# RWKV output normalisation as its own chain in a hand-ordered weave, with attention, gate and output work taken off the raised priority

## The chip, the cores and the metric

One core of one Trainium2 chip runs the whole program. The metric is device time in microseconds (us) per execution, the median of three runs. Before the change it is 2834.69 us (2834.21 to 2839.68).

## What is computed

Two layers of a Conformer-style block on 512 tokens of width 1024, all in float32: a SwiGLU feed-forward, a mixing sub-layer, and a second feed-forward. The mixing sub-layer adds three gated branches: RWKV-7 (8 heads of 64), gated linear attention, and 4-head attention to a fixed memory. The part that matters here is the RWKV head recurrence and its output:

```
def step(state, inp):
    r_t, w_t, k_t, v_t, kk_t, a_t = inp
    sa = einsum('bhvk,bhk->bhv', state, -kk_t)
    state = state * w_t + sa * (kk_t * a_t) + v_t * k_t
    return state, einsum('bhvk,bhk->bhv', state, r_t)
mean = y.mean(-1); var = mean((y - mean) ** 2)
yn = (y - mean) * rsqrt(var + RWKV_LN_EPS) * ln_w + ln_b
out = (yn + sum(r * k * r_k, -1) * v) * g
...
merged = einsum('bsjc,jcd,bsjd->bsd', branches, w_branch, sigmoid(u_gate))
x = x + merged @ w_out
```

## The kernel before

Activations lie with channels on the 128 partitions and 512 tokens along the free axis. Every large weight tile is loaded as float32 (`wraw`), split by ScalarE into a high part `whi` (L180) and by VectorE into a low part `wlo` (L181), and each product is three 128x128 by 128x512 matmuls (high-high, high-low, low-high). In the mixing sub-layer these stand on L295 (`pieces`).

The RWKV core is chunked: 64 tokens a chunk, four chunks a **half**, two halves for each of four **head pairs**, so eight halves (numbered 0 to 7 below) in each of two layers. A half passes through four stages:

- *gates* (`rwkv_gates`): for the first half of a pair a norm over the keys (`ksq`, L379 on TensorE, square root L387, reciprocals L397), then two small products (L382), tanh (L384, L385) and the factors `kk`, `a`, `G` (L388 to L399).
- *first* (`rwkv_first`): the factors `AR`, `KB` (L426 to L432), score products (L444), masks (L449), start of a triangular inverse.
- *inverse* (`rwkv_inverse`): rounds of VectorE transpose `X` (L521), product (L528), mask `W` (L531), product (L536), sum into `Z` (L537).
- *second* (`rwkv_second`): the state recurrence over the four chunks. Each chunk goes through three products with a hand-over after each: L580 then `qs` (L581, VectorE); L586 then `VU` (L587/L588, ScalarE); L592 then the state `S` (L598, VectorE, two halves of 64 rows). After four chunks the outputs are formed (L608) and added into `y` (L613, twice).

Then comes the output part, which is the same generator's tail: sum and mean of `y` (L616, L617), subtraction (L618), square on ScalarE (L620), sum (L622), an inverse square root by three Newton steps in 14 small GpSimd instructions (L624 to L631), multiplication into `y` (L632). After a pause in the order, TensorE transposes `y` (L638) and forms the output gate (L639), and ScalarE and VectorE finish (L641 to L649).

`weave` writes TensorE's order by hand. It keeps a running clock `now` in ns; each generator yields the TensorE time of what it just issued and a latency, and is not asked again until `now` has passed that latency plus a slack of 400. In between, `stream` supplies the large matmuls of the other two branches and of the projections, one at a time at 227 ns. Generators are asked in a fixed order: second, inverse, first, gates, attention heads. TensorE executes exactly this order. The other engines' orders come from a scheduler that sorts what is ready by priority; all the chains are issued under `high_priority(offset=100000)`, the large stream is not. Each engine then runs its list strictly in order, so an instruction that waits holds everything behind it.

The pause after the normalisation is `yield 5 * 218, 7500` (L634). Because the tail belongs to `rwkv_second`, the next half's recurrence begins only after this half's transposes.

Of the kernel before, what the change touches and what calls it, by code (L numbers as in the profile page):

```python
# [19 lines left out]
P = 128  # L20
# [59 lines left out]
class Net:  # L80
# [322 lines left out]
    def rwkv_first(self, hp, hf, r, k, v, kk, kh, a, G):  # L403
        nc, rw, t1 = self.nc, self.rw, self.t256
        N = 256
# [60 lines left out]
            nc.scalar.activation(by(AB[rows, :, rows]), ab, AF.Copy)  # L466
            nc.scalar.activation(by(AU[rows, :, rows.start // 2:rows.start // 2 + 32]), ab[:, :, :, 32:64], AF.Copy)
        nc.vector.tensor_tensor(Z, A4, self.c("eye").unsqueeze(1).to_broadcast([P, 4, 64]), ALU.add)
        rk = t1("t1", 2)
        nc.vector.scalar_tensor_tensor(rk, r, self.pcol("r_k", hp), kh, ALU.mult, ALU.mult)  # L470
        self.freed = 2 * hp + hf + 1
        yield 8 * 218, 3600
# [37 lines left out]
        bv = t1("bv", 2)  # L510
# [51 lines left out]
    def rwkv_second(self, hp, hf, E, AR, VU, u0, GR, Z, KBT, bv):  # L562
        nc, rw, t1 = self.nc, self.rw, self.t256
        N = 256
        cs = slice(hf * N, (hf + 1) * N)
        hc = slice(hp * P, (hp + 1) * P)
        y = t1("y")
        for c in range(4):
            g = hf * 4 + c
            p, par = c // 2, c % 2  # L570
# [39 lines left out]
        for par in range(2):  # L610
            rows = slice(par * 64, par * 64 + 64)
            yv = y[rows].rearrange("p (h t) -> p h t", h=4)
            nc.vector.tensor_tensor(yv, psy[rows].rearrange("p (h e t) -> p h e t", h=4, e=2)[:, :, par, :], yv, ALU.add)  # L613
        y4 = y.rearrange("p (h t) -> p h t", h=4)
        st = rw.tile([P, 4], F32, name="st", tag="st", bufs=2)
        nc.vector.reduce_sum(st, y4, AX.X)  # L616
# [13 lines left out]
            nc.gpsimd.tensor_scalar(tt, tt, -0.5, 1.5, ALU.mult, ALU.add)  # L630
            nc.gpsimd.tensor_tensor(rt, rt, tt, ALU.mult)  # L631
        nc.vector.tensor_tensor(y4, y4, rt.unsqueeze(2).to_broadcast([P, 4, 64]), ALU.mult)  # L632
        self.seconds = 2 * hp + hf + 1
        yield 5 * 218, 7500  # L634

        ps = self.small("f")
        for q in range(2):
# [2 lines left out]
        y = t1("t2", 2)  # L640
# [12 lines left out]
    def weave(self, rkv0, gl, restore, xa):  # L653


        now, slack = 0, 400
        ready, rkv, gated, query = {0: 3500}, {0: rkv0}, {}, {}
        self.inv, self.sec, inverted = {}, {}, 0
        self.freed = self.seconds = self.tails = 0

        def first_gates():
            for n in range(8):
                while n // 2 not in rkv or ready[n // 2] > now or self.freed < n:
                    yield None
                gated[n] = yield from self.rwkv_gates(n // 2, n % 2, *rkv[n // 2])

        def first():
            for n in range(8):
                while n not in gated or self.seconds < n - 1:
                    yield None  # L670
                yield from self.rwkv_first(n // 2, n % 2, *gated.pop(n))

        def inverse():
            nonlocal inverted
            for n in range(8):
                while n not in self.inv:
                    yield None
                yield from self.rwkv_inverse(*self.inv.pop(n))
                inverted = n + 1

        def second():
            for n in range(8):
                while n not in self.sec or inverted <= n:
                    yield None
                yield from self.rwkv_second(n // 2, n % 2, *self.sec.pop(n))
                self.tails = n + 1

        def heads():
            for j in range(2, 4):
                while j not in query:  # L690
                    yield None
                yield from self.xa_head(xa[0], j, query[j], *xa[1:])
                ready[-j] = 0

        def rest():
            part = self.branch_g(1, *gl, True, range(KD))
            query[2] = yield from self.xa_query(xa[0], 2)
            yield None
            for cost in part:
                yield cost  # L700
                if cost is None and 3 not in query and -2 in ready:
                    query[3] = yield from self.xa_query(xa[0], 3)
                    yield None
            yield from self.branch_g(2, *restore(), False, range(KD))
            early = [self.keep.tile([P, 4 * NMEM], F32, name="early", tag=n) for n in ("kT", "vm")]
            for m in range(4):
                gates.append((yield from self.gate_g(0, m, early[m // 2][:, (m % 2) * T:(m % 2 + 1) * T])))
                yield None

        def stream():  # L710
            fill = rest()
            for hp in range(1, 4):
                while self.freed < 2 * hp:
                    cost = next(fill)
                    while cost is not None:
                        yield cost
                        cost = next(fill)
                rkv[hp] = yield from self.rwkv_rkv(hp)
                ready[hp] = now + 3500
            for cost in fill:  # L720
                if cost is not None:
                    yield cost

        gates = []
        parts = [[g, 0] for g in (second(), inverse(), first(), first_gates(), heads())]
        big = stream()
        ends = 0
        while parts or big is not None:
            for part in parts:
                if part[1] > now:  # L730
                    continue
                try:
                    with self.tc.high_priority(offset=100000):
                        step = next(part[0])
                except StopIteration:
                    parts.remove(part)
                    break
                if step is not None:
                    now += step[0]
                    part[1] = now + step[1] + slack  # L740
                    break
            else:
                if big is None:
                    now = min(part[1] for part in parts) if parts else now
                    ends += 1
                    assert ends < 100
                    continue
                try:
                    now += next(big)
                except StopIteration:  # L750
                    big = None
        return gates
# [382 lines left out]
```

## Time and profile before

| | us |
|---|---|
| median of the runs | 2834.69 |
| the profiled execution's own time | 2841.49 |
| its span, first to last instruction | 2839.6 |
| around the span (2841.49 - 2839.6) | 1.9 |
| weave of layer 1 of 2, from the key norm to the last transpose | 588 to 960 |
| weave of layer 2 of 2, same | 1998 to 2364 |

The profile's sections give each engine's busy time, the chain that ended last, and groups of instructions by source line; PE is TensorE, DVE is VectorE, ACT is ScalarE and POOL is GpSimd. In the views of waits, a row reads "who <- for whom: us in total, times, longest". In the views by stretch, each row has the length, the busy time of each engine with its instruction count, and the granted share of the TensorE clock. A small float32 matmul in the program appears as two records in the trace, because it is run in two passes.

### The profile page before, as it was taken

To read this page: it belongs to the slowest core of one execution; us is meant where nothing else is said; L and a number is where in the kernel's file an instruction comes from. 1 tells how busy PE (TensorE), PEld (TensorE's weight loads), DVE (VectorE), ACT (ScalarE), POOL (GpSimd) and SP (SyncE) were. 2 spreads that over 40 slices of the span, in tenths; PEclk is the share of its full clock that TensorE was granted. 3 is DMA by queue.
4 is the path that set the end of the run, shared out by engine and by line. 5 is a ranking of instruction groups with operands and counts; after the bars stand their busy time and mean duration, and the time that the engine had idled before them with its cause. 6 is when DMAs were issued, how large, how long until landed. Compare 5 with 4: busy or idle time off the path is not lost.

```text
span 2839.6 us, 35473 instructions
## 1 busy us (share of the span) xinstructions
PE 2737.2 (96%) x13280; PEld 2247.1 (79%) x13280; DVE 1617.8 (57%) x2993; ACT 1152.3 (41%) x2079; POOL 72.6 (3%) x342
## 2 busy tenths in 40 slices
PE   8999999998989999999999999999999899999998
PEld 6888887777777788888888888877777688888886
DVE  6434446777677654444454344567777775544444
ACT  5323345554343443323343233465544334432332
POOL 0000000001010000000000000000010110000000
PEclk9999999999899999999999999999999999999999
DMA  5232332211111232232332323312111113322222
GB/s 184 93 99 97 106 133 79 93 54 60 53 53 51 98 123 96 89 104 97 97 111 87 106 97 111 127 67 90 66 54 58 60 54 101 118 97 92 102 92 87
DMA packets 91723, 258.04 MB, mean 91 GB/s; under 512 B 10464, under 2 KB 24832, under 8 KB 91552
## 3 DMA queue, kind: packets, MB, share of 16 engines
q1 hardware_dynamic: 91552, 255.79, 26.8%
q8 instruction: 104, 1.70, 0.2%
q14 instruction: 67, 0.55, 0.1%
HBM read 243.69 MB, written 12.06 MB: 90 GB/s over the span
## 4 chain that ended last, share of the span: by engine, by line
PE 88%; DVE 6%; ACT 2%; POOL 2%; issue 2%; DMA 0%; SPq 0%; DVEq 0%; POOLq 0%; ACTq 0%
PE ps_b L295 21%; PE ps_b L196 19%; PE ps_b L198 19%; PE ps_b L197 18%; PE ps_c L528 2%; PE ps_c L536 1%; DVE wlo L181 1%; PE ps_i L444 1%; PE ps_f L794 1%; PE ps_f L586 1%; PE ps_f L816 1%; DVE knrm L397 0%; POOL tt L628 0%; ACT whi L180 0%; PE ps_y L932 0%
## 5 line engine op out<-in xcount | busy, mean ns | idle before, releaser
L180 ACT ACTIVATE whi<-wraw 128x512 fp32r<-128x512 f32 (+1 forms) x874 | 544.0, 623 | 1165.2 <-PE ps_b L197 901.6
L181 DVE TENSOR_TENSOR wlo<-wraw,whi 128x512 fp32r<-128x512 f32 (+1 forms) x874 | 589.9, 676 | 483.7 <-ACT whi L180 475.6
L196 PE MATMUL ps_b<-xhi,whi 128*128 128x512 f32 x1424 | 556.2, 391 | 9.9 <-ACT xhi L206 7.7
L198 PE MATMUL ps_b<-xhi,wlo 128*128 128x512 f32 x1424 | 555.8, 390 | 0.1
L197 PE MATMUL ps_b<-xlo,whi 128*128 128x512 f32 x1424 | 555.8, 390 | 0.0
L295 PE MATMUL ps_b<-xhi,wlo 128*128 128x512 f32 x864 | 353.6, 409 | 12.9 <-DVE wlo L181 12.9
L295 PE MATMUL ps_b<-xlo,whi 128*128 128x512 f32 x864 | 355.7, 412 | 0.0
L295 PE MATMUL ps_b<-xhi,whi 128*128 128x512 f32 x864 | 351.1, 406 | 1.8 <-DVE gc L945 1.2
L196 PEld LDWEIGHTS ps_b<-xhi,whi 128*128 128x128 f32 x1424 | 266.5, 187 | 67.0 <-ACT xhi L206 7.7
L198 PEld LDWEIGHTS ps_b<-xhi,wlo 128*128 128x128 f32 x1424 | 266.5, 187 | 57.9 <-DVE wlo L181 0.8
L197 PEld LDWEIGHTS ps_b<-xlo,whi 128*128 128x128 f32 x1424 | 266.6, 187 | 57.5 <-DVE xlo L207 0.5
L196 PE MATMUL ps_b<-mhi,whi 128*128 128x512 f32 x704 | 277.5, 394 | 0.0
L198 PE MATMUL ps_b<-mhi,wlo 128*128 128x512 f32 x704 | 276.0, 392 | 0.0
L197 PE MATMUL ps_b<-mlo,whi 128*128 128x512 f32 x704 | 273.3, 388 | 0.0
L295 PEld LDWEIGHTS ps_b<-xhi,wlo 128*128 128x128 f32 x864 | 165.7, 192 | 48.0 <-DVE wlo L181 15.9
L295 PEld LDWEIGHTS ps_b<-xhi,whi 128*128 128x128 f32 x864 | 165.6, 192 | 40.1 <-issue 5.6
L295 PEld LDWEIGHTS ps_b<-xlo,whi 128*128 128x128 f32 x864 | 165.8, 192 | 31.6 <-issue 1.8
L198 PEld LDWEIGHTS ps_b<-mhi,wlo 128*128 128x128 f32 x704 | 132.1, 188 | 30.9
L197 PEld LDWEIGHTS ps_b<-mlo,whi 128*128 128x128 f32 x704 | 132.2, 188 | 29.5
L196 PEld LDWEIGHTS ps_b<-mhi,whi 128*128 128x128 f32 x704 | 132.3, 188 | 26.3
L271 DVE TENSOR_TENSOR fm<-ps_b,ft 128x512 f32<-128x512 f32 x88 | 60.9, 692 | 126.9 <-PE ps_b L198 126.9
L267 DVE TENSOR_TENSOR ft<-ps_b,rs 128x512 f32<-128x512 f32 x88 | 60.9, 692 | 126.0 <-PE ps_b L198 125.8
(299 smaller groups left out, 3334.2 us busy)
## 6 DMA issues: line engine op xcount, KB each, us to landing
wraw<-in_ffn_in_dram SPq DMA_DIRECT2D x176, 512.0 KB, 3.4
wraw<-in_w_main_dram SPq DMA_DIRECT2D x108, 512.0 KB, 3.5
wraw<-in_ffn_out_dram SPq DMA_DIRECT2D x64, 512.0 KB, 3.5
wraw<-in_ffn_out_dram SPq DMA_DIRECT2D x64, 192.0 KB, 2.3
wraw<-in_w_branch_dram SPq DMA_DIRECT2D x48, 256.0 KB, 2.5
wraw<-in_w_out_dram SPq DMA_DIRECT2D x16, 512.0 KB, 3.4
xd<-x SPq DMA_DIRECT2D x16, 256.0 KB, 2.2
wraw<-in_w_k_dram SPq DMA_DIRECT2D x8, 512.0 KB, 3.6
```

Source lines behind the costliest of these rows:

```text
L180: nc.scalar.activation(hi, r, AF.Copy)
L181: nc.vector.tensor_tensor(lo, r, hi.bitcast(F32), ALU.subtract)
L196: nc.tensor.matmul(ps, a[0], b[0], start=start, stop=False)
L197: nc.tensor.matmul(ps, a[0], b[1], start=False, stop=False)
L198: nc.tensor.matmul(ps, a[1], b[0], start=False, stop=stop)
L267: nc.vector.tensor_tensor(t, pp[0], rs, ALU.mult)
L271: nc.vector.tensor_tensor(m, pp[1], t, ALU.mult)
L295: self.nc.tensor.matmul(ps, w[k][a], xs[k][b], start=k + i == 0, stop=k == n - 1 and i == 2)
L444: nc.tensor.matmul(pss[j][:, c * P:(c + 1) * P], KBc[js, c, :], AR[js, c, :], start=True, stop=True)
L528: nc.tensor.matmul(ps[:, u, :], AB[:, u, :], X[:, u, :], start=True, stop=True)
L536: nc.tensor.matmul(ps[:, u, :], W[:, u, :], Z[:, u, :], start=True, stop=True)
L586: nc.tensor.matmul(psu[:, :P], Z[:, 2 * p:2 * p + 2, :].rearrange("p j t -> p (j t)"), qs, start=True, stop=True)
```

## The change

The tail of `rwkv_second` from the first sum onward becomes a generator `rwkv_out`, and a new loop `outputs()` in the weave drives it. The pause before the transposes becomes `yield 0, 12000`. Second of the next half no longer waits for this half's transposes; it waits for those of the half before (`self.tails < n - 1`), and `y` gets two buffers. The loops carry a priority offset each: second, inverse and first keep 100000, gates, attention heads and outputs get 0, which is issue order. The very first gates become due 6000 instead of 3500 after the start. The tile `t1` goes from two buffers to one. No instruction is added or removed. Line numbers after the change: the lines of `rwkv_second` up to L613 become one lower, the tail's L616 to L632 become L624 to L640, L638/L639 become L645/L646, and attention's L794 becomes L809.

```
-        rk = t1("t1", 2)
+        rk = t1("t1")
...
-        y = t1("y")
+        y = t1("y", 2)
...
+        self.out[2 * hp + hf] = y, bv
+        yield 5 * 218, 0
+
+    def rwkv_out(self, hp, hf, y, bv):
...
-        self.seconds = 2 * hp + hf + 1
-        yield 5 * 218, 7500
+        yield 0, 12000
...
-        ready, rkv, gated, query = {0: 3500}, {0: rkv0}, {}, {}
+        ready, rkv, gated, query = {0: 6000}, {0: rkv0}, {}, {}
...
-                while n not in self.sec or inverted <= n:
+                while n not in self.sec or inverted <= n or self.tails < n - 1:
                     yield None
                 yield from self.rwkv_second(n // 2, n % 2, *self.sec.pop(n))
+                self.seconds = n + 1
+
+        def outputs():
+            for n in range(8):
+                while n not in self.out:
+                    yield None
+                yield from self.rwkv_out(n // 2, n % 2, *self.out.pop(n))
                 self.tails = n + 1
...
-        parts = [[g, 0] for g in (second(), inverse(), first(), first_gates(), heads())]
+        parts = [[g, 0, p] for g, p in ((second(), 100000), (inverse(), 100000), (first(), 100000), (first_gates(), 0),
+                                        (heads(), 0), (outputs(), 0))]
...
-                    with self.tc.high_priority(offset=100000):
+                    with self.tc.high_priority(offset=part[2]):
```

Three places show what the edit does to the engines' lists, all in the first layer.

TensorE around the transposes of half 0, before. Here `ksq` and `wlal` are the gates of half 2, and L295 the large stream:

```order
L295 MATMUL ps_b<-yh,whi 128x512
L295 MATMUL ps_b<-yl,whi 128x512
L379 MATMUL ps_i<-ksq,cst 128x512
L382 MATMUL ps_i<-wlal,wz 128x256 x2
L638 MATMUL ps_f<-cst,y 128x128 x2
L639 MATMUL ps_f<-sgl,g_1111 128x256
L295 MATMUL ps_b<-yh,wlo 128x512
L295 MATMUL ps_b<-yh,whi 128x512
```

The same transposes after, between the recurrence products of half 1 (L579 on chunk 2, L585):

```order
L415 MATMUL ps_i<-cst,v 128x128 x2
L295 MATMUL ps_b<-xhi,wlo 128x512
L295 MATMUL ps_b<-xhi,whi 128x512
L295 MATMUL ps_b<-xlo,whi 128x512
L579 MATMUL ps_y<-S_106,AR 128x128
L645 MATMUL ps_f<-cst,y 128x128 x2
L646 MATMUL ps_f<-sgl,g_1111 128x256
L295 MATMUL ps_b<-xhi,wlo 128x512
```

Between the last output product of half 0 and its transposes stood 27 large matmuls and three small steps (L554, L379, L382); now 40 large ones and, besides those three, two chunks of half 1's recurrence.

VectorE around the multiplication of half 0, before; the `t` names are numbered copies of tile `t2`, `knrm` and `sg` belong to the gates of half 2:

```order
L618 TENSOR_TENSOR y<-y,st 128x256
L181 TENSOR_TENSOR wlo<-wraw,whi 128x512
L622 TENSOR_REDUCE st<-t_5266 128x4
L953 TENSOR_TENSOR gs<-ps_b,rs 128x512
L181 TENSOR_TENSOR wlo<-wraw,whi 128x512
L632 TENSOR_TENSOR y<-y,rt 128x256
L395 TENSOR_SCALAR knrm<-knrm 128x256 x2
L397 RECIPROCAL knrm<-knrm 128x128 x2
L388 TENSOR_SCALAR sg<-sg 128x256
```

After, the stretch that ends with it (L640); the sum L630 that the GpSimd steps wait for stands 16 rows ahead of L640:

```order
L397 RECIPROCAL knrm<-knrm 128x128
L427 TENSOR_TENSOR AR<-rk_r,E 128x2x2x64
L470 SCALAR_TENSOR_TENSOR t_5509<-rk_r,par_78,t_5352 128x256
L597 SCALAR_TENSOR_TENSOR S_106<-S_107,E,ps_f 64x64 x2
L431 TENSOR_TENSOR KB<-t_5352,G 128x2x64 x2
L398 TENSOR_TENSOR kk<-kk,knrm 128x256
L640 TENSOR_TENSOR y<-y,rt 128x256
L426 SCALAR_TENSOR_TENSOR AR<-kk,E 128x2x128
L580 TENSOR_TENSOR qs_108<-ps_y,u_5026 64x128
```

The gates and the first stage of half 2 and the recurrence of half 1 have moved in between the sum and the multiplication.

VectorE between the second output add of half 1 and the first sum of its normalisation, before; `W` is the mask step of half 2's inverse:

```order
L576 COPY qs_108<-u_5584 64x128
L181 TENSOR_TENSOR wlo<-wraw,whi 128x512
L613 TENSOR_TENSOR y<-ps_y,y 64x256 x2
L531 TENSOR_TENSOR W<-ps_c,cst 128x512
L616 TENSOR_REDUCE st<-y 128x4
```

After, the list from behind the two adds (L612) to the sum (L624); `AR`, `KB` are half 3's factors, `t_5599`, `Z`, `X` the inverse of half 2, `t_5525` and `A_5499` its inputs:

```order
L426 SCALAR_TENSOR_TENSOR AR<-kk,E 128x2x128
L427 TENSOR_TENSOR AR<-rk_r,E 128x2x2x64
L489 TENSOR_TENSOR t_5599<-ps_i,A_5499 128x128
L431 TENSOR_TENSOR KB<-t_5525,G 128x2x64
L490 TENSOR_TENSOR Z<-Z,t_5599 128x64x2
L431 TENSOR_TENSOR KB<-t_5525,G 128x2x64
L491 TENSOR_TENSOR t_5599<-ps_i,Z 128x64
L432 SCALAR_TENSOR_TENSOR KB<-a,G 128x2x128
L492 TENSOR_TENSOR Z<-Z,t_5599 128x64
L575 COPY qs_108<-u_5597 64x128
L521 STREAM_TRANSPOSE X<-Z 128x256
L624 TENSOR_REDUCE st<-y 128x4
```

One row stood between add and sum, and eleven stand there now. Further down, three rows stand between the last sum (L622, now L630) and the multiplication of this half in both programs, and the inverse's `Z` (L537) comes behind the multiplication in both. On TensorE, the transposes of half 1 had 19 large matmuls between them and the last output product and now have 33.

More of the change, by code (lines that the diff above doesn't have):

```diff
@@ L565, in rwkv_second @@
         cs = slice(hf * N, (hf + 1) * N)
-        hc = slice(hp * P, (hp + 1) * P)
-        y = t1("y")
+        y = t1("y", 2)
         for c in range(4):
@@ L613, in rwkv_second @@
             nc.vector.tensor_tensor(yv, psy[rows].rearrange("p (h e t) -> p h e t", h=4, e=2)[:, :, par, :], yv, ALU.add)
+        self.out[2 * hp + hf] = y, bv
+        yield 5 * 218, 0
+    def rwkv_out(self, hp, hf, y, bv):
+        nc, rw, t1 = self.nc, self.rw, self.t256
+        N = 256
+        cs = slice(hf * N, (hf + 1) * N)
+        hc = slice(hp * P, (hp + 1) * P)
         y4 = y.rearrange("p (h t) -> p h t", h=4)
@@ L656, in weave @@
         now, slack = 0, 400
-        ready, rkv, gated, query = {0: 3500}, {0: rkv0}, {}, {}
-        self.inv, self.sec, inverted = {}, {}, 0
+        ready, rkv, gated, query = {0: 6000}, {0: rkv0}, {}, {}
+        self.inv, self.sec, self.out, inverted = {}, {}, {}, 0
         self.freed = self.seconds = self.tails = 0
```

## The prediction

> **What bounds the kernel now.** First the page:
>
> ```profile
> span 2839.6 us, 35473 instructions
> PE 2737.2 (96%) x13280; PEld 2247.1 (79%) x13280; DVE 1617.8 (57%) x2993; ACT 1152.3 (41%) x2079; POOL 72.6 (3%) x342
> ```
>
> TensorE has work for 96% of the span, and no instruction is added or removed. All that the change can win or lose is the time in which TensorE stands still or runs slowly. The view by stretch shows where that is:
>
> ```profile
> 585.00:970.00 385.00, 349.06 (x1988) 291.62 (x1989) 266.74 (x653) 161.15 (x383) 31.19 (x140) 0.95 0.18 58
> 970.00:1030.00 60.00, 60.00 (x266) 49.56 (x265) 35.34 (x56) 23.57 (x38) 0.00 (x0) 1.00 0.34 114
> 1993.00:2375.00 382.00, 349.99 (x2015) 289.94 (x2015) 275.67 (x664) 162.95 (x387) 31.23 (x140) 0.97 0.19 62
> ```
>
> The columns are length, busy PE, PEld, DVE, ACT, POOL with counts, then the granted clock. The two weaves leave TensorE idle for 385 - 349.1 = 35.9 and 382 - 350.0 = 32.0 us, 68 together; the stretch behind the first is full. The clock also sinks to 0.95 and 0.97, worth at most 0.05 x 385 + 0.03 x 382 = 31 us. So about 99 us is the most that any order of the weaves could give. The second row also gives the pace: 60 / 266 = 0.226 us a large matmul. TensorE's waits name the causes:
>
> ```profile
> PE ps_f L638 <- DVE y L632: 41.2, 16, 6.1
> PE ps_b L295 <- DVE wlo L181: 15.9, 8, 3.6
> ...
> PE ps_i L379 <- ACT ksq L376: 3.9, 1, 3.9
> ```
>
> The transposes wait in all 16 halves. What they wait for is seen on VectorE in half 0 of the second layer, with GpSimd and TensorE beside it:
>
> ```profile
> 2070.51 0.42 DVE L613 TENSOR_TENSOR y<-ps_y,y 64x256 f32<-64x256 f32 x1 [0.39 <-PE ps_y L608]
> ...
> 2075.46 0.42 DVE L622 TENSOR_REDUCE st<-t 128x4 f32<-128x256 f32 x1
> 2076.61 0.69 DVE L953 TENSOR_TENSOR gs<-ps_b,rs 128x512 f32<-128x512 f32 x1 [0.72 <-PE ps_b L295]
> 2077.21 0.68 DVE L181 TENSOR_TENSOR wlo<-wraw,whi 128x512 fp32r<-128x512 f32 x1
> 2080.22 0.43 DVE L632 TENSOR_TENSOR y<-y,rt 128x256 f32<-128x256 f32 x1 [2.32 <-POOL rt L631]
> ```
>
> ```profile
> 2076.05 0.19 POOL L624 TENSOR_SCALAR st<-st 128x4 f32<-128x4 f32 x1 [4.83 <-DVE st L622]
> ...
> 2079.99 0.20 POOL L631 TENSOR_TENSOR rt<-rt,tt 128x4 f32<-128x4 f32 x1
> ```
>
> ```profile
> 2069.34 1.06 PE L608 MATMUL ps_y<-VU,GR 128*128 128x128 f32 x8
> 2070.24 0.56 PE L554 MATMUL ps_c<-Z,w 128*128 128x64 f32 x4
> ...
> 2076.86 1.02 PE L379 MATMUL ps_i<-ksq,cst 128*128 128x512 f32 x2
> 2077.73 1.02 PE L382 MATMUL ps_i<-wlal,wz 128*128 128x256 f32 x4
> 2080.79 0.41 PE L638 MATMUL ps_f<-cst,y 128*128 128x128 f32 x2 [2.04 <-DVE y L632]
> ```
>
> From the end of L608 (2070.24) to the end of L632 (2080.65) the normalisation takes 10.4 us, 4.1 of them the 14 GpSimd steps. The order put only 2080.79 - 2.04 - 2070.24 = 8.5 us of work in between. Hence 2.0 us of waiting. The row also shows that VectorE itself stood held at L632 for 2.3 us, with the recurrence and the weight splits queued behind it. A second bound is near: VectorE is busy 267 of 385 us.
>
> **The change, step by step.** *The transposes' waits (41.2).* Half 0 gets 13 more large matmuls (13 x 0.226 = 2.9) and seven recurrence products at 0.225 (four L608 take 2070.24 - 2069.34 = 0.90), 1.6: 4.5 us more room. The other halves get 11 to 20 more large ones, at least 2.5 us. The longest gap is 6.1, the mean 41.2 / 16 = 2.6. If the chain kept its length, nearly all 41.2 would go. It does not: its VectorE rows lose their priority. At half 1, eleven rows of other chains now stand between add and sum. Their sizes:
>
> ```profile
> L521 DVE STREAM_TRANSPOSE X<-Z 128x256 f32<-128x256 f32 x32 | 14.0, 439 | 0.7
> L431 DVE TENSOR_TENSOR KB<-t,G 128x128 f32<-128x128 f32 x16 | 3.9, 280 | 0.0
> L432 DVE SCALAR_TENSOR_TENSOR KB<-a,G 128x256 f32<-128x256 f32 x8 | 3.3, 411 | 0.0
> ```
>
> At 0.28 to 0.44 each, about 11 x 0.32 = 3.5 us, against 14 x 0.226 = 3.2 us of new room: half 1 keeps its gap. I leave 2.5 us to half 1, 1.5 to halves 3 and 5, nothing to the rest: 5.5 a layer, 11 in all. This step: -30 (bounds -41 and 0).
>
> *The splits behind the gates (15.9).* After a gate step the large stream waits for `wlo`, since the raised gates go first; with the gates in issue order part goes, but L640 holding VectorE does the same to the splits. I take -4 (bounds -16 and +4).
>
> *The first gates.* L379 comes ten large matmuls later, 2.3 of its 3.9 us: -2.3 (bounds -3.9 and 0).
>
> *What is late next.* Half 1's recurrence now runs right behind half 0's, while VectorE works on half 2's gates and first stage. Between half 1's state updates of chunks 1 and 2, VectorE's new list holds KB twice, L398, L640, L426, `qs`, L399, an output add, L432, KH, the two closing steps of half 0, two reciprocals and three splits. The rows:
>
> ```profile
> L181 DVE TENSOR_TENSOR wlo<-wraw,whi 128x512 fp32r<-128x512 f32 x69 | 46.9, 685 | 14.3 <-ACT whi L180 9.8 <-PE ps_b L295 3.1 <-PE ps_f L592 1.2
> L397 DVE RECIPROCAL knrm<-knrm 128x128 f32<-128x128 f32 x16 | 14.2, 924 | 0.0
> L598 DVE SCALAR_TENSOR_TENSOR S<-S,E,ps_f 64x64 f32<-64x64 f32 x48 | 13.4, 279 | 11.1 <-PE ps_f L592 10.7
> L632 DVE TENSOR_TENSOR y<-y,rt 128x256 f32<-128x256 f32 x8 | 3.4, 425 | 22.3 <-POOL rt L631 22.3
> ```
>
> Three splits 2.1, two reciprocals 1.8, KH and the add at the split's size 1.4, eight of the size of L632 3.0 (the two KB taken as one), `qs` and the two state rows at 0.28 0.8: 9.1 us. TensorE's list has, from chunk 1's L592 to the product that needs chunk 2's state, 17 large matmuls (3.8) and some 15 small ones at 0.22 (3.3): 7.1. So the state comes 2.0 us late there. Nothing in the trace shows this crowd, since the recurrence of a pair's second half began only after a pause; the bounds are 0 and, if all 16 halves meet it twice, 64 us. I count two such places in each of three pairs a layer, 12 x 2.2 = 26, the value nearest to the sum just made.
>
> *Clock.* Fewer long gaps, more short ones: -3 of the 31 (bounds -25 and +10). The buffer counts cost nothing: `t1` is written again only after L509 of the half before, which the order keeps ahead of it, and the second `y` is what lets the recurrence go on. What the gates put on ScalarE now falls beside a recurrence; ScalarE is idle 385 - 161 = 224 us of the weave, and I count it within the 2.2.
>
> Sum: -30 - 4 - 2 + 26 - 3 = -13 us. On the profiled execution's 2841.5 that is 2828.5. That execution lay 6.8 us above the median of the runs, so the median goes from 2834.7 to about 2822.
>
> **Two rules and their rows.** VectorE and GpSimd disturb each other: the first of the 14 steps takes 0.19 us above, and beside a run of VectorE instructions
>
> ```profile
> 844.57 1.71 POOL L624 TENSOR_SCALAR st<-st 128x4 f32<-128x4 f32 x1 [7.33 <-DVE st L622]
> ```
>
> 1.71 us. [...] That speaks against this change, which fills VectorE just while GpSimd iterates; by it the six odd halves with a gap would pay up to 1.5 us each, 9 in all, and the sum would be -4. I keep it inside the range, since the waits between such instructions are many.
>
> The clock falls after gaps far below the 6.1:
>
> ```profile
> 888.79 0.53 PE L638 MATMUL ps_f<-cst,y 128*128 128x128 f32 x2 [1.57 <-DVE y L632]
> ```
>
> ```profile
> 889.00:892.40 3.40, 3.40 (x14) 3.13 (x13) 1.85 (x6) 0.56 (x1) 0.20 (x1) 0.50 0.01 2
> ```
>
> [...]
>
> **Rivals.** *The waits just go.* VectorE absorbs the crowd, the transposes' 41 and half the splits' 16 vanish with no new wait, and the clock recovers 15: 2834.7 - 66 = 2769. For it: VectorE is idle 31% of the weave. Against it: the idle time lies in the pauses that the change closes.
>
> *VectorE becomes the bound (slower).* Place: the second half of each pair, from its first state update to its last product, with the next pair's gates beside it. Price: 2.2 us at each place; the change loses from 12 + 13 / 2.2 = 18 places on. If the crowd also meets half 0 of each pair and the inverse behind it, 24 places cost 53, and the time is 2834.7 - 39 + 53 = 2849. For it: the profile's VectorE rows already add to 267 us in a weave that would be about 15 us denser. Against it: the most crowded rows carry raised priority.
>
> *The change only moves the waits.* The normalisation is as late as before in the odd halves, and `X` and `qs` wait where L638 did: within 5 us, 2831.
>
> **How the numbers follow.** Forecast 0.42, waits go 0.15, moved only 0.18, slower 0.25. Faster by over 0.2% (5.7 us, about what a measurement of this kernel can tell from no change): 0.42 + 0.15 = 0.57; within: 0.18; slower: 0.25. The range runs from 2796, the forecast's gains without its price (2834.7 - 39), to 2849; most of the first rival lies outside it.
>
> **What would show it.** The row of waits of the transposes (L645 on L640) should fall from 41 to about 11, and stand at half 1 with 2 to 4 us. New rows should appear for the recurrence and the inverse on `S`, `qs`, `X` or `W`, 26 us together. The idle part of the weaves should go from 68 to about 58 us, with the clock at 0.95 to 0.98. If those new rows stay under 10 us, the first rival holds; if they pass 40, the second.

## The result, and the profile after

The changed kernel takes 2860.03 us (median of 6 runs, 2857.08 to 2867.60) beside 2840.62 for the kernel before (6 runs, 2834.21 to 2845.95, among them the three that stand ahead of the prediction): a ratio of 1.0072, 95% interval 1.0051 to 1.0093. It is slower, and outside the range. The profiled execution has a span of 2857.7 us, 18.1 more than before:

```profile
span 2857.7 us, 35465 instructions
PE 2753.5 (96%) x13280; PEld 2258.7 (79%) x13280; DVE 1621.5 (57%) x2993; ACT 1153.7 (40%) x2080; POOL 73.6 (3%) x342
```

TensorE's busy time rose from 2737.2 to 2753.5 with the same 13280 records; its idle time went from 102.4 to 2857.7 - 2753.5 = 104.2. So 16.3 of the 18.1 us are not waiting but the same work done more slowly. The view by core says by what: the mean granted clock fell from 0.985 to 0.980, which is (1 - 0.985) x 2839.6 = 42.6 us lost before and 0.020 x 2857.7 = 57.2 after.

```profile
core 0: 2857.7 us, clock 0.980
```

By stretch (same columns as in the prediction), the weave of layer 1 hardly changed, and that of layer 2 lost clock. TensorE's idle time in the two is 31.8 + 36.4 = 68 us, as before, and not the 58 that were forecast:

```profile
585.00:970.00 385.00, 353.17 (x2013) 294.06 (x2012) 271.22 (x658) 162.57 (x386) 31.96 (x140) 0.96 0.18 61
970.00:1030.00 60.00, 60.00 (x266) 49.50 (x265) 35.25 (x55) 23.67 (x38) 0.00 (x0) 1.00 0.34 114
1993.00:2375.00 382.00, 345.65 (x1920) 285.37 (x1919) 266.58 (x646) 155.84 (x374) 31.25 (x139) 0.92 0.16 55
```

TensorE's waits (who <- for whom: total, times, longest) are others than before:

```profile
PE ps_f L585 <- DVE sg L656: 16.6, 6, 3.3
PE ps_b L295 <- DVE wlo L181: 9.8, 6, 2.1
...
PE ps_f L645 <- DVE y L640: 7.6, 4, 3.1
PE ps_c L528 <- DVE X L521: 7.3, 5, 2.5
...
PE ps_f L585 <- DVE qs L580: 4.1, 4, 1.6
PE ps_i L350 <- DVE GR L449: 3.5, 2, 2.1
PE ps_f L585 <- DVE y L653: 3.5, 2, 1.7
PE ps_f L591 <- ACT pr L815: 3.5, 2, 1.7
PE ps_y L579 <- DVE S L597: 3.3, 3, 2.0
```

The transposes' waits went from 41.2 to 7.6, the splits' from 15.9 to 9.8. At the top now stands a wait that was not there: L585, the recurrence's second product, for `sg` of L656 and `y` of L653, 20.1 us together. These two are the last VectorE instructions of the output part, and `qs`, which L585 multiplies, has nothing to do with them. What they share is a buffer. `small("f")` is one PSUM tile (`bufs=1`): the transposes (L645) and the gate (L646) are written to `ps_f`, L653 or L656 is its last reader, and L585 writes the same tile next. The timeline of the first such place, TensorE and then VectorE (a number in brackets is the wait ahead of the row, and for whom):

```profile
677.64 0.41 PE L645 MATMUL ps_f<-cst,y 128*128 128x128 f32 x2 [0.46 <-DVE y L640]
677.88 0.60 PE L646 MATMUL ps_f<-sgl,g 128*128 128x256 f32 x2
678.13 0.58 PE L295 MATMUL ps_b<-xhi,wlo 128*128 128x512 f32 x1
678.55 0.40 PE L295 MATMUL ps_b<-xhi,whi 128*128 128x512 f32 x1
682.28 0.76 PE L585 MATMUL ps_f<-qs,Z 128*128 128x128 f32 x2 [3.34 <-DVE sg L656]
```

```profile
680.79 0.42 DVE L649 TENSOR_TENSOR t<-t,bv 128x256 f32<-128x256 f32 x1
681.12 0.68 DVE L181 TENSOR_TENSOR wlo<-wraw,whi 128x512 fp32r<-128x512 f32 x1
681.72 0.41 DVE L656 TENSOR_TENSOR sg<-t,ps_f 128x256 f32<-128x256 f32 x1
```

From the gate product to the release pass about 3.6 us. In the order of the kernel before, 14, 14, 13 and 14 large matmuls (3 us) stood between the gate product and the next `ps_f` write in halves 0, 2, 4 and 6, since the recurrence began only when the tail's last `yield 218 + 432, 1500` was over. In the changed order there stand 2, 5, 0 and 0. These are the eight places of the two rows.

### The profile page after: what moved, and what is told of

The parts are those of the page before. It is cut to its first block, busy times and chain, and to the rows that moved or that the text cites. A ratio compares the mean times of both kernels' runs of the same rounds, so it can differ in the third digit from the quotient of the medians.

```text
span 2857.7 us, 35465 instructions
## 1 busy us (share of the span) xinstructions
PE 2753.5 (96%) x13280; PEld 2258.7 (79%) x13280; DVE 1621.5 (57%) x2993; ACT 1153.7 (40%) x2080; POOL 73.6 (3%) x342
## 4 chain that ended last, share of the span: by engine, by line
PE 88%; DVE 5%; ACT 3%; issue 2%; POOL 1%; DMA 0%; SPq 0%; DVEq 0%; ACTq 0%; POOLq 0%
PE ps_b L295 21%; PE ps_b L196 19%; PE ps_b L198 18%; PE ps_b L197 18%; PE ps_c L528 2%; PE ps_c L536 1%; PE ps_i L444 1%; PE ps_f L809 1%; PE ps_f L585 1%; DVE wlo L181 0%; PE ps_f L831 0%; PE ps_f L591 0%; PE ps_y L947 0%; PE ps_i L479 0%; PE ps_y L579 0%
## 5 line engine op out<-in xcount | busy, mean ns | idle before, releaser
L295 PE MATMUL ps_b<-xhi,wlo 128*128 128x512 f32 x864 | 356.1, 412 | 9.8 <-DVE wlo L181 9.8
L295 PE MATMUL ps_b<-xhi,whi 128*128 128x512 f32 x864 | 354.7, 411 | 1.9 <-DVE gc L960 1.2
L295 PE MATMUL ps_b<-xlo,whi 128*128 128x512 f32 x864 | 356.2, 412 | 0.0
L198 PEld LDWEIGHTS ps_b<-xhi,wlo 128*128 128x128 f32 x1424 | 266.5, 187 | 57.7 <-DVE wlo L181 0.7
L295 PEld LDWEIGHTS ps_b<-xhi,wlo 128*128 128x128 f32 x864 | 166.7, 193 | 44.7 <-DVE wlo L181 12.6
L295 PEld LDWEIGHTS ps_b<-xhi,whi 128*128 128x128 f32 x864 | 166.5, 193 | 40.1 <-issue 6.4
L295 PEld LDWEIGHTS ps_b<-xlo,whi 128*128 128x128 f32 x864 | 166.8, 193 | 30.9 <-issue 1.8
```

The lines of the kernel that those rows point to most:

```text
L198: nc.tensor.matmul(ps, a[1], b[0], start=False, stop=stop)
L295: self.nc.tensor.matmul(ps, w[k][a], xs[k][b], start=k + i == 0, stop=k == n - 1 and i == 2)
```

## The experiments

Each ratio is to the kernel before on the same chip. "Idle" is span less TensorE's busy time in the run's profile. "Clock" is (1 - clock) x span, averaged over the kernel's runs.

| | us, median | ratio (95%) | idle | clock |
|---|---|---|---|---|
| before (65 runs beside the experiments) | 2841.6 | 1 | 102.4 | 43.1 |
| changed | 2860.0 | 1.0072 (1.0051 to 1.0093) | 104.2 | 57.7 |
| e1 changed, again (one run) | 2866.1 | | 104.0 | 65.9 |
| e2 ScalarE copies the gate | 2849.2 | 1.0029 (1.0014 to 1.0044) | 98.9 | 50.3 |
| e3 outputs raised | 2859.8 | 1.0065 (1.0044 to 1.0086) | 109.7 | 51.9 |
| e4 all raised | 2864.5 | 1.0079 (1.0056 to 1.0101) | 119.0 | 45.3 |
| e5 recurrence held back | 2823.3 | 0.9934 (0.9909 to 0.9959) | 87.6 | 33.3 |
| e6 before, gates lowered | 2837.3 | 0.9980 (0.9965 to 0.9995) | 93.9 | 43.7 |
| e7 before, longer pause | 2841.6 | 0.9994 (0.9982 to 1.0007) | 103.2 | 48.0 |
| e8 changed, waits filled | 2855.2 | 1.0043 (1.0024 to 1.0062) | 90.4 | 44.4 |
| e9 before, pause and gates | 2830.6 | 0.9957 (0.9936 to 0.9978) | 92.5 | 38.5 |
| e10 before, two Newton steps | 2817.1 | 0.9919 (0.9889 to 0.9949) | 86.7 | 32.6 |
| e11 e5 with two Newton steps | 2813.6 | 0.9901 (0.9866 to 0.9937) | 80.8 | 29.3 |
| e12 e9 with two Newton steps | 2820.6 | 0.9932 (0.9905 to 0.9958) | 84.9 | 34.9 |

My theory after the result was *release*: L585 waits for a buffer that the output part reads late. The rivals were *crowd* (VectorE has too many instructions there in any order) and, for the time rather than the waits, *clock*.

### e1: the changed kernel again

> The changed kernel once more, unaltered, for a second profile. In the first profile TensorE was idle for 104.2 us of the span (102.4 before the change) while its clock was halved for 117.5 us in all (85.6 before): 16 us of the 18 come from the clock. If the halved stretches follow from where the gaps lie, idle time and halved time both repeat: 104 +- 1 and 117 +- 4 us. If they are chance from execution to execution, the idle time repeats and the halved time moves by more than 10 us, and the time with half of that.

The idle time repeated to 0.2 us, 104.0 beside 104.2; the clock did not:

```profile
core 0: 2864.3 us, clock 0.977
```

The clock records of the first profile add up to 117.5 us at half speed, those of the second to 134.6. At half speed one large matmul starts 0.43 us behind another (at 683.27 and 683.70 in the first profile) and elsewhere 0.226, so about half of the time is lost: by that the difference is worth some 8.5 us, an estimate, and the span is 6.6 longer. Of the two expectations the second came true. So in these two profiles what TensorE waited for was fixed by the program, and how much clock the waits cost varied from execution to execution. That explains nearly all of a kernel's spread: the 65 runs of the kernel before went from 2832.9 to 2860.3 us, and with the clock's loss taken off each of them lies at 2794 to 2802. The six of the changed kernel, 2857.1 to 2867.6, lie at 2801.7 to 2805.7. At full clock the change costs about 4 us (means 2803.1 and 2798.9); the other 15 are clock.

### e2: ScalarE reads the gate out of PSUM

```
             yo = t1("sg")
-            nc.vector.tensor_tensor(yo, y, ps[:, N:], ALU.mult)
+            nc.scalar.activation(yo, ps[:, N:], AF.Copy)
+            nc.vector.tensor_tensor(yo, y, yo, ALU.mult)
```

The branch that writes `y3` has the same edit.

> The changed kernel, with the output gate copied out of PSUM by ScalarE right behind its normalisation step, so that the single ps_f buffer no longer waits for two VectorE instructions. Theory 'release' (the recurrence's L585 stands behind the output's two late readers of ps_f, 16.6 + 3.5 us): these two rows fall from 20 to under 6 us, and the time by 14 us or more, to 2835 to 2847. Rival 'crowd' (VectorE is full there, and the recurrence would be late anyway): the waits come back as waits for qs, VU and S, and the time stays within 5 us of 2860.

It went down by 11 us (0.4% by the ratios), short of the 14 and far from the rival's 5. L585's waits for the output fell from 20.1 to 12.6, not under 6, because ScalarE is late too: at half 4 the copy waited for the tile `sg`, which VectorE still read for the gates.

```profile
845.60 0.56 ACT L648 ACTIVATE t<-ps_f,par 128x256 f32<-128x256 f32 x1 [0.61 <-PE ps_f L646]
846.07 0.46 ACT L385 ACTIVATE a<-ps_i,half 128x256 f32<-128x256 f32 x1
847.26 0.38 ACT L658 ACTIVATE sg<-ps_f 128x256 f32<-128x256 f32 x1 [0.73 <-DVE G L390]
```

The splits' waits rose from 9.8 to 19.8. The wait follows whoever reads the buffer last, from VectorE's pass (20.1) to ScalarE's copy (12.6): that speaks for the release theory without settling it.

### e3 and e4: priorities put back

```
-                                        (heads(), 0), (outputs(), 0))]
+                                        (heads(), 0), (outputs(), 100000))]
```

> The changed kernel with the outputs back at the raised priority, gates and attention left in issue order. Theory 'release': the output's last two VectorE instructions go ahead of the others, the waits of L585 for them fall from 20 to under 10 us, and the time goes to 2845 to 2852. Rival 'crowd': it is the number of VectorE instructions, not their order, that makes things late; the waits change rows but not their sum, and the time stays at 2855 to 2865.

e4 raises `first_gates` and `heads` as well.

> The changed kernel with every chain back at the raised priority: only the moves are left (own chain for the outputs, pause 12000, first gates later). If the lower priorities are the cause, the time goes back to 2840 or under, with the splits' waits back at 14 to 16 us. If the overlap of the recurrence with the outputs is the cause (release), the time stays at 2850 to 2865.

e3 measured 2859.8: my number was wrong, and that of *crowd* came true. With the outputs raised, L585 still waits 15.0 + 3.5 us for their readers, so their priority is not what makes them late. e4 rules the lowered priority out as the cause of the loss: with everything raised the kernel is as slow or slower, and TensorE idles for 119.0 us. The splits' waits went to 12.9 (14 to 16 expected); the changed order was already worse, and the lower priorities took 15 us of idle time off it. The loss comes from the moves; with the clock's loss taken off, e4's runs average 2818.7 us, 20 above the kernel before.

### e5: the recurrence held back behind the transposes

In the loop of `weave`, `sec` being the generator `second()`, and `self.hold` set by `rwkv_out` ahead of its last yield:

```
                     part[1] = now + step[1] + slack
+                    if self.hold:
+                        self.hold = False
+                        for q in parts:
+                            if q[0] is sec:
+                                q[1] = max(q[1], now + 2800 + slack)
```

> The changed kernel, with one thing put into the order: behind the transposes of an output the recurrence is not asked again for 3200, so that 12 to 15 large matmuls stand between the transposes and the next L585 in every half, where the changed kernel has 0 to 5 in the even halves and the kernel before 13 or 14. Theory 'release': the waits of L585 for the outputs' readers (20 us) fall under 3, the idle time of the two weaves from 68 to 46 to 54 us, and the time to 2830 to 2845. Rival 'crowd': the recurrence waits elsewhere instead (qs, VU, S over 20 us together), and the time stays within 5 us of 2860.

2823.3 us, 1.4% less than the changed kernel by the ratios (0.9934 / 1.0072), and faster than the kernel before. Nothing but TensorE's order, and with it the lists of the other engines, differs. The waits for the output's readers are gone from the profile:

```profile
PE ps_b L295 <- DVE wlo L181: 22.4, 10, 3.8
...
PE ps_c L528 <- DVE X L521: 5.8, 3, 2.5
PE ps_f L645 <- DVE y L640: 5.0, 4, 2.1
PE ps_y L579 <- DVE S L597: 3.8, 5, 1.9
```

```profile
585.00:970.00 385.00, 359.12 (x2072) 299.55 (x2072) 278.60 (x672) 168.64 (x395) 30.94 (x140) 0.98 0.19 64
1993.00:2375.00 382.00, 355.76 (x2052) 294.64 (x2051) 279.20 (x663) 162.12 (x383) 31.18 (x139) 0.98 0.19 65
```

The idle part of the weaves is 25.9 + 26.2 = 52 us (46 to 54 expected), and the crowd's waits did not rise. VectorE is busier than in either kernel (279 of 385 us), so it is not the bound. Of the 36 us by which it beats the changed kernel, some 12 remain with the clock's loss taken off (means 2803.1 and 2790.9); the other 24 are clock. This settles it between *release* and *crowd*, by distance: no run gave `ps_f` a second buffer, which would be the most direct test. What was left over went partly into the splits (9.8 to 22.4).

### e6, e7 and e9: the parts of the change on the old order

e6 gives gates and attention the offset 0 in the kernel before, TensorE's order unchanged. e7 does only this:

```
-        yield 5 * 218, 7500
+        yield 5 * 218, 12000
```

> The kernel before, with gates and attention taken off the raised priority and nothing else: TensorE's order is the same to the last row. If lowering is what gains in this change (all raised, the changed kernel had 83 us idle in its weaves, against 68), the splits' waits fall from 15.9 to under 11 and the idle time of the weaves from 63 to 50 to 58: 5 to 12 us faster than before. If the lowered chains make the recurrence and the inverse wait, it is within 4 us of before or slower.

> The kernel before, with the pause of 7500 made 12000 and nothing else, so that 6 to 28 more large matmuls stand ahead of each half's transposes, and the recurrence still begins behind them. By the sum of the prediction for this step alone, the transposes' waits go from 41 to under 12 us with no new wait, and with the clock the time falls by 30 to 45 us. If the later recurrence costs the inverse or the gates what it saves, the time falls by less than 10.

> The kernel before with both the longer pause of 12000 and the lowered gates and attention, but no chain of its own for the outputs. Alone, the pause turned the transposes' waits into splits' waits (43.5 us), because 12 us of raised gate rows stand ahead of a split on VectorE. If that is the reason, the lowered gates now let the splits go first: splits' waits under 20 us, idle time of the weaves 45 to 52, time 2815 to 2830, no worse than the changed kernel with the recurrence held back (2823). If the separate chain is what allows the gain, it stays at 2832 to 2842.

e6: the splits' waits fell from 15.9 to 8.2 and the idle time by 8.5 us; the time by 0.2% (0.05 to 0.35), some 6 us of 2841, at the low end of the 5 to 12 that I expected, with an interval from 1 to 10.

e7 is the sharpest miss. The transposes' waits vanished from the profile, and the kernel gained 0.06%, which its interval doesn't tell from nothing. The 41.2 us came back in other rows, 27.6 of them in the splits (from 15.9), 8.5 in `X` (from 1.2) and the rest in smaller ones:

```profile
PE ps_b L295 <- DVE wlo L181: 43.5, 12, 7.2
PE ps_c L528 <- DVE X L521: 9.7, 10, 2.3
```

TensorE's idle time went from 102.4 to 103.2.

VectorE's list at half 4 of layer 1 shows how. It is held for GpSimd at L632, then the raised gates run, and the splits come last:

```profile
841.08 0.42 DVE L632 TENSOR_TENSOR y<-y,rt 128x256 f32<-128x256 f32 x1 [3.94 <-POOL rt L631]
...
846.90 1.75 DVE L397 RECIPROCAL knrm<-knrm 128x128 f32<-128x128 f32 x2
...
851.23 1.28 DVE L181 TENSOR_TENSOR wlo<-wraw,whi 128x512 fp32r<-128x512 f32 x2
```

```profile
851.96 0.80 PE L295 MATMUL ps_b<-xhi,wlo 128*128 128x512 f32 x1 [6.17 <-DVE wlo L181]
```

The kernel before had its 6.1-us gap at the same place, under the transposes' name; there the raised gates ran first and the hold for GpSimd came behind them:

```profile
850.51 0.66 PE L638 MATMUL ps_f<-cst,y 128*128 128x128 f32 x2 [6.11 <-DVE y L632]
```

The row of a wait names what stands first in TensorE's list; the cause was VectorE.

e9 joins the two: 2830.6, just above what I expected, with 31.2 us of splits' waits (under 20 expected). Beside e6, which has 36.1 us of transposes' waits where e9 has none, it idles only 1.4 us less (92.5 and 93.9): with the gates lowered too, the pause moves the waits more than it removes them. e9 gains 0.43% without a chain of its own, from lowered gates and pause together; e5, with the chain, gained 0.66%. The intervals overlap, and what the separate chain adds is not settled by them.

### e8: useless work in the waits

```
+            if self.fill and g:
+                self.fill = False
+                for _ in range(3):
+                    nc.tensor.matmul(psq[:, 2 * P:], self.c("ident"), Z.rearrange("p j t -> p (j t)")[:, :2 * P],
+                                     start=True, stop=True)
             psu = self.small("f")
```

`self.fill` is set where an output's transposes have been issued.

> The changed kernel with three useless 128x256 matmuls put ahead of the first L585 behind each output's transposes (their result is not used). They do nothing but keep TensorE busy, 1 to 2 us in each place, 8 of the places inside a wait of 1.7 to 3.3 us. Theory 'clock' (of the 18 us that the change lost, 16 are halved clock, which follows a 3.4 us window in which TensorE was busy for less than about half): the idle time falls by 10 us or more, the halved time by 15 to 40 us, and the kernel gets faster by 5 to 15 us although it does more work. If the clock has nothing to do with the gaps, the time rises by what the fillers take outside a wait, 0 to 12 us.

The fillers took 22.0 us of TensorE:

```profile
L587 PE MATMUL ps_y<-Z,cst 128*128 128x256 f32 x84 | 22.0, 400 | 0.1
```

The idle time fell by 13.8 us, so the fillers cost 8 us net. The measured ratio still went down, from 1.0072 to 1.0043, and the clock's loss from 57.7 to 44.4 us on average. A kernel with 22 us more work is 5 us faster by the medians and 8 by these ratios (0.29% of 2841). The two intervals overlap (1.0051 to 1.0062), so the gain in time is not settled; the clock's own numbers are what supports the clock theory: 0.982 to 0.986 in the nine runs of e8, 0.977 to 0.982 in the six of the changed kernel.

### e10, e11 and e12: a shorter GpSimd chain

```
-        for _ in range(3):
+        for _ in range(2):
```

One refinement of the inverse square root is left out, 4 of the 14 GpSimd instructions.

> The kernel before with two Newton steps of the inverse square root instead of three (one step of the refinement is left out), so 10 GpSimd instructions instead of 14. If the 43.0 us for which VectorE is held on GpSimd in the 16 halves set the wait, the hold falls by 16 x 1.1 = 18 us, the transposes' waits from 41 to 23 to 26, and the time by 15 to 28 us. If VectorE is late there for other reasons, the waits fall by less than 8 us.

> The changed kernel with the recurrence held back behind the transposes and two Newton steps instead of three (one step left out). VectorE was held for 23.4 us on GpSimd with three. If the hold is what makes the remaining splits (22 us) and transposes (5 us) wait, both fall, together to under 17 us, and the time goes from 2823 to 2805 to 2818. If the crowd of VectorE instructions does, the time stays within 5 us of 2823.

> The kernel before with the pause of 12000, the lowered gates and two Newton steps instead of three (one step left out). If pause, priority and GpSimd hold are all that matters, it is as fast as the held changed kernel with two steps, 2800 to 2820. If the separate chain has a worth of its own, it is over 8 us slower than that.

e10: 0.8% faster, about 23 us of 2841, inside the 15 to 28 expected; VectorE's hold at L632 fell from 43.0 to 33.5 (25 expected) and the transposes' waits from 41.2 to 22.7. e11: 2813.6, inside its 2805 to 2818; the splits' and the transposes' waits are 16.2 + 4.5 (under 17 expected). But VectorE's hold did not fall in it, 23.7 us beside 23.4 in e5, and the intervals of e5 and e11 overlap: what the shorter chain is worth behind the held recurrence is not shown. In e12 the hold is 34.1 us beside 35.6 in e9. e12 is just above its range, 7 us behind e11, under the 8 that I had set for a worth of the chain. The interval of e10 alone reaches from 0.9889 to 0.9949, so the order of these three is open; that each beats the kernel before is not.

## Why the prediction was wrong, point by point

*The transposes' waits, -30.* The row fell by 33.6, and where it stayed was foreseen:

```profile
708.51 0.69 PE L645 MATMUL ps_f<-cst,y 128*128 128x128 f32 x2 [2.59 <-DVE y L640]
```

That is half 1, forecast at 2.5 us (3.08 in layer 2). But as a saving the step is refuted: in e7 the same row fell by 41 and the time by nothing that the interval shows. I treated the gap as a distance on TensorE to be filled with matmuls. It was VectorE's time, taken by the hold for GpSimd and by raised rows, and TensorE met it at the next instruction that needed VectorE. e10 shortened the hold itself, and the time followed.

*The splits, -4.* 15.9 to 9.8, within the bounds; e6 gives 8.2 from the lowered gates alone.

*The first gates, -2.3.* 3.9 to 1.6: right to the digit, and nothing beside the rest.

*What is late next, +26.* This is the step that failed in its mechanism. It put the price on chunk 2's state (L579 and L825 on S: 4.9 us in the trace) and on VectorE's list. The largest new wait, 20.1 us, is on the PSUM buffer `ps_f`. The rows and orders that I had shown have L638 and L639 writing `ps_f` and the recurrence moved next to them; I asked what every product reads, and never what it overwrites and who must have read that. The part on buffers looked only at `t1` and `y`, whose counts the diff edits. The other new rows (`X` 6.1 more than before, `qs` 3.4 more, `GR` 3.5, `pr` 3.5, S 4.6 more, smaller ones 5) make 26 between them. That this is the forecast's number is luck: the rows that it had named (S, `qs`, `X`, `W`) make only 14 of it. The release came on top: some 46 in place of 26. (The price of 2.2 us a place was also not the 2.0 of the sum ahead of it; twelve places at 2.0 make 24.)

*Clock, -3.* The miss is nearly as large, 17.6 us beside the 20 of the new waits: +14.6 in the profiles and in the means. No run shows the -3 or its bounds; what the runs showed in their place is this +14.6. I took the longest gaps going (6.1 to 3.3) as a gain. But half clock came with the gaps of 2 to 3 us too: in the profile of the changed kernel, of the sixteen gaps of 2.0 to 3.34 us in the weaves 13 had a halved stretch begin during them or within 3.5 us of their end, and one more lay in such a stretch. The change took away six gaps of 3.5 to 6.1 us, but left the weaves with sixteen of 2 to 3.34 where there had been nine, and with nine of 1.5 to 2 where there had been two, some of them close together.

*Sum.* Waits: -33.6 - 6.1 - 2.3 + 46 = +4, beside +1.8 of idle time measured. With the clock +16 to +19: the 18.1 of the profiles.

*The rivals.* New waits passed the 40 us that I had set for the slower rival, but neither by its mechanism (VectorE as the bound: e5 has VectorE busier and TensorE faster) nor at its 2849.

*GpSimd beside VectorE.* Of the +9 us that were weighed, the trace shows nothing: GpSimd is busy 73.6 us after and 72.6 before, and the longest of its 14 steps takes 0.74 us after and 1.71 before. VectorE's own rows beside the step of 1.71 us took 0.42 us (L426, L427), the medians of these lines, so that VectorE was disturbed in its turn is not shown.

## What to carry to other kernels

Before moving a chain, list for each of its products not only the inputs but the buffer that it writes and the last reader of what is in it: a yield that looks like a latency may be all that keeps two users of a single buffer apart. Read a row of waits from the other side too: where the engine waited for is itself held, more work in front of the wait can merely hand it to the next instruction in the queue; test it by lengthening the distance alone, as e7 does (41.2 us of waits gone from one row, 102.4 us of idle time and then 103.2). And split a small difference into idle time and clock before explaining it: they need different remedies.

## What the runs showed of the hardware

The clock records of two profiles, the kernel before and the changed one, show shares of 1.0 and 0.5 and nothing between. The shortest of them is 3413 ns long. The starts of the halved stretches lie at multiples of 3413.33 ns from one another, to within 5 ns over the whole span, and the grid of these multiples lies differently against the first instruction in each profile (1.87 and 2.05 us from it to the grid line before). TensorE's busy share in each window of that grid, in both profiles together and 10 us away from the ends of the span:

| window | busy | windows | followed by a halved one |
|---|---|---|---|
| at full clock | under 40% | 20 | 20 |
| | 40 to 50% | 10 | 7 |
| | 50 to 70% | 28 | 5 |
| | 70% and more | 1543 | 0 |
| at half clock | under 80% | 9 | 9 |
| | 80 to 90% | 2 | 1 |
| | 90% and more | 41 | 10 |

What a gap costs by these counts is an estimate. One of 2.1 us inside one window leaves it (3.41 - 2.1) / 3.41 = 38% busy; all 20 such windows were followed by a halved one, in which half of 3.41 us is lost, 1.7. Cut in the middle by a grid line, it leaves two windows 69% busy; of that kind 5 in 28 were followed by a halved one. A second gap of over 0.7 us in the halved window leaves that under 80% busy, and all 9 such were followed by another halved one. Layer 2 of the changed kernel shows such a row of windows around the waits of 2.1 us (at 2259) and 2.4 us (at 2270), nearly on the grid:

```profile
2254.40:2257.80 3.40, 2.94 (x15) 1.98 (x14) 3.29 (x10) 1.58 (x5) 2.50 (x12) 1.00 0.07 23
2257.80:2261.20 3.40, 1.30 (x7) 0.78 (x6) 3.38 (x8) 1.65 (x5) 0.44 (x3) 0.97 0.00 0
2261.00:2264.40 3.40, 3.27 (x10) 2.43 (x11) 2.54 (x7) 0.00 (x0) 0.00 (x0) 0.50 0.00 0
...
2267.80:2271.20 3.40, 2.56 (x8) 1.47 (x6) 2.88 (x8) 2.60 (x8) 0.20 (x1) 0.50 0.04 13
2271.20:2274.60 3.40, 1.86 (x6) 1.60 (x7) 3.40 (x9) 0.57 (x3) 0.00 (x0) 0.50 0.29 103
2274.60:2278.00 3.40, 3.40 (x15) 2.36 (x15) 2.23 (x6) 1.05 (x2) 0.11 (x1) 0.50 0.45 154
```

The window with 1.30 us of work is followed by five halved ones: two in which TensorE is all but full, then two that its next wait leaves at 75% and 55%, and one more.

What stays open: why the changed kernel's gaps meet the grid worse than the old ones on average. Away from the ends of the span its first profile starts 17 halved stretches and extends them by 12 windows in all, the one of before 13 and by 8; that the gaps stand closer together fits this, but no run varied their distance alone.
